# Half-token products after Strassen's scheme in a gated feed-forward block

## The chip, the cores and the metric

One core of a Trainium2 chip runs the whole program. The metric is the device time of one execution in microseconds. The engines that matter are TensorE (PE, with its weight loads, PEld), VectorE (DVE), ScalarE (ACT) and SyncE (SP), which issues nearly all DMAs from one queue.

## What is computed

A decoder trunk of one layer: 512 tokens, width 1024. Four attention branches are mixed and added to `x`; then comes the part that is changed:

```python
def conv_ffn(xn, w_up, conv_w, conv_b, w_down):
    hdn = xn @ w_up                               # 512 x 1024 times 1024 x 5632
    hp = jnp.pad(hdn, ((0, 0), (CONV_W - 1, 0), (0, 0)))
    acc = conv_b
    for j in range(CONV_W):                       # causal, over tokens, width 3
        acc = acc + conv_w[j] * hp[:, j:j + s_len]
    g, u = jnp.split(acc, 2, axis=-1)
    return (jax.nn.gelu(g, approximate=False) * u) @ w_down   # 512 x 2816 times 2816 x 1024
x = x + conv_ffn(rmsnorm(x, norm_ffn_g), ...)
return rmsnorm(x, norm_final_g)
```

## The kernel before, in words

Everything is held transposed: channels on the 128 partitions, the 512 tokens on the free axis. A float32 product is made of float32r parts: each operand is split into a high part (a cast, on ACT) and a low part (raw minus high, on DVE), and a product is three matmuls, high by high, high by low and low by high.

**The weight stream.** All big weights are entries of one list, `stream`, in the order in which PE wants them. `emit_weight` (L93) loads an entry of up to 128x1024 into a raw buffer (tag `wr`, two buffers, DMA on SP) and splits it into a high and a low tile (tags `wh` and `wl`, three buffers each) with `split_weight` (L89: cast on ACT, subtract on DVE). `weight()` (L106) returns the next entry and emits entries until two beyond it are there. Emitted weights get a priority 60 instructions ahead of their place.

**Order of the work.** PE's instructions stay in the order of the program. Those of the other engines are placed by a planner by priority, which is the place in the program, and by readiness: a ready instruction may pass one that waits. The buffers of one tag, though, are handed out in the order in which the program asks for them, each as soon as any buffer of the tag is free, which is when all that use the tile in it are done.

**Up projection** (44 tiles of 128 output channels). `up_tile(i)` (L798) runs 24 matmuls of 512 columns (L120: eight blocks of contraction times three) into a PSUM bank (tag `a`, six banks), DVE multiplies by the norm's factor into `h` (L805, two buffers), ACT makes the first tap and the bias (`cv`, L807, three buffers), DVE adds two taps (L809). Tiles come in pairs, gate and value: ACT takes the gate's gelu (L815), DVE multiplies (L817), and ACT and DVE split the product into `mh` and `ml` (L818, L819), which hold 22 blocks for the down projection.

**Down projection** (8 tiles). For each, `weight(3, 1)` gives the 22 blocks of contraction in entries of 8, 8 and 6 (`DCH`), and `down` (L829) runs 66 matmuls of 512 columns (L833). DVE adds the result to `x1` (L854), ACT squares it (L856), DVE sums the squares in `accf` (L858), ACT applies the gain (L859). The last tile runs in two halves of 256 tokens, 66 matmuls of 256 columns each. `last_norm` (L839) makes each half's factor from the squares and multiplies the outputs (L845), which four DMAs a half write (L846). That of the first half is issued within the second half's matmuls.

Of the kernel before, what the change touches and what calls it, by code (L numbers as in the profile page):

```python
# [44 lines left out]
def fr(ap):  # L45
    return ap.bitcast(F32)
# [3 lines left out]
def trunk(ctx: ExitStack, tc: tile.TileContext, xt, wv0, wv, wp, wdk, wg, wb, wo, wu, wd,  # L50
          convp, foxb, t5, onehot, consts, ymask, out):
    nc = tc.nc
    V, A, G, T, SP = nc.vector, nc.scalar, nc.gpsimd, nc.tensor, nc.sync
# [3 lines left out]
    wpool = ctx.enter_context(tc.tile_pool(name="wpool", bufs=WBUFS))  # L57
    xpool = ctx.enter_context(tc.tile_pool(name="xpool", bufs=1))
# [28 lines left out]
    stream, ready = [], []  # L87
# [90 lines left out]
    with ExitStack() as ph:  # L178
# [23 lines left out]
        rstd = cp.tile([P, S], F32, name="rstd0")  # L202
# [32 lines left out]
        for c, (a, b) in list(enumerate(CHUNKS))[1:]:  # L235
            sq = hp.tile([P, 2, S], F32, name=f"sq{b}", tag="sq", bufs=4)
# [46 lines left out]
        for tt in range(NB):  # L283
            jk = pp.tile([P, P], F32, name=f"jk{tt}", tag="ot")
            V.tensor_tensor_reduce(out=jk, in0=rstd[:, tt * P:(tt + 1) * P], in1=ident, scale=1.0, scalar=0.0,
                                   op0=OP.mult, op1=OP.add, accum_out=rst[:, tt:tt + 1])
        for tt in range(NB):
# [3 lines left out]
                            op0=OP.mult)  # L291
# [87 lines left out]
        with tc.issue_after(last_lo):  # L379
# [16 lines left out]
                             op0=OP.mult, op1=OP.add)  # L396
        ch = pp.tile([P, 2, S], F32R, name="ch", tag="hi", bufs=HB)
# [241 lines left out]
        for pr in ("F0", "S0", "F1", "S1", "M0", "M1", "D0", "D1"):  # L639
            nm, b = pr[0], "FMSD".index(pr[0])  # L640
            for h in (2 * int(pr[1]), 2 * int(pr[1]) + 1):
                q = lambda pr=pr: qk[pr + "q"]
                if nm == "D":
                    k, v = (lambda: kD[:, 0]), (lambda: vvD[:, :, 0])
                else:
                    k = lambda pr=pr, hh=h % 2: qk[pr + "k"][:, hh]
# [3 lines left out]
                else:  # L650
                    bias = fox_bias if nm == "F" else t5_bias(h + 4 * (nm == "D"), nm == "D")
# [115 lines left out]
        for f in range(KT):  # L767
            ps = bank(f"o{f}")
# [25 lines left out]
    mh = p3.tile([P, ND, S], F32R, name="mh")  # L794
    ml = p3.tile([P, ND, S], F32R, name="ml")
    rstd = None

    def up_tile(i):  # L798
        nonlocal rstd
        ps = bank(f"u{i}")  # L800
        drive(dense_steps(ps, *weight(), blocks_of(xhi), blocks_of(xlo), late=(i == 0)))
        if i == 0:
            rstd = rms_rstd(mean_square([acc], "mso"), S, "f", p3)
        h = p3.tile([P, S], F32, name=f"h{i}", tag="h", bufs=2)
        V.tensor_tensor(out=h, in0=ps, in1=rstd, op=OP.mult)  # L805
        c = p3.tile([P, S], F32, name=f"cv{i}", tag="cv", bufs=3)
        A.activation(c, h, AF.Identity, scale=cvp[:, i, 2:3], bias=cvp[:, i, 3:4])  # L807
        for x in (1, 2):
            V.scalar_tensor_tensor(out=c[:, x:], in0=h[:, :S - x], scalar=cvp[:, i, 2 - x:3 - x], in1=c[:, x:],  # L809
                                   op0=OP.mult, op1=OP.add)  # L810
        return c

    for j in range(ND):
        g = up_tile(2 * j)
        last_gelu = A.activation(g, g, AF.Gelu)  # L815
        u = up_tile(2 * j + 1)
        V.tensor_tensor(out=u, in0=g, in1=u, op=OP.mult)  # L817
        A.copy(mh[:, j], u)  # L818
        V.tensor_tensor(out=ml[:, j], in0=u, in1=fr(mh[:, j]), op=OP.subtract)  # L819
    with tc.issue_after(last_gelu.ins):  # L820
        A.preload_act_table_set("natural_log_exp_and_others")

# [3 lines left out]
    accf = p3.tile([P, S], F32, name="accf")  # L826
    full = slice(0, S)

    def down(ch, o, cs, late=False):  # L829
        blocks = [(hi[:, k], lo[:, k], k0 + k) for (hi, lo), (k0, c) in zip(ch, DCH) for k in range(c)]  # L830
        for n, (hi, lo, k) in enumerate(blocks):
            for m, (a, b) in enumerate(((hi, mh), (hi, ml), (lo, mh))):
                T.matmul(o, a, b[:, k, cs], start=(n == 0 and m == 0), stop=(n == ND - 1 and m == 2))  # L833
            if n % 4 == 3:
                yield

    msf = [None, None]

# [7 lines left out]
            (SP if q % 2 == 0 else A).dma_start(out[:, 2 * q:2 * q + 2, hs[h]], xs)  # L846

    for f in range(KT):
        ch = weight(3, 1)
        gf = gn[:, 2 * KT + f:2 * KT + f + 1]  # L850
        if f < KT - 1:
            ps = bank(f"dn{f}")
            drive(down(ch, ps, full))
            V.tensor_tensor(out=x1[f], in0=ps, in1=x1[f], op=OP.add)  # L854
            sq = p3.tile([P, S], F32, name=f"sqd{f}", tag="h", bufs=2)
            A.activation(accf if f == 0 else sq, x1[f], AF.Square)  # L856
            if f:
                V.tensor_tensor(out=accf, in0=accf, in1=sq, op=OP.add)  # L858
            A.activation(x1[f], x1[f], AF.Copy, scale=gf)  # L859
# [20 lines left out]
CHUNKS = ((0, 1), (1, 2), (2, 4), (4, 6), (6, 8))  # L880
WARM = 9
NV0 = 328
DCH = ((0, 8), (8, 8), (16, 6))
# [109 lines left out]
```

## Time and profile before

| | us |
|---|---|
| median of 3 runs | 857.08 (856.91 to 857.58) |
| the profiled execution | 857.41 |
| its span in the profile | 855.6 |
| PE busy | 837.3 |
| up projection, PE | 483.3 to 723.2 |
| down projection, PE | 723.2 to 845.4 |

The span runs from the first to the last instruction in the trace; the execution's own time has some 1.8 us around it. A line of a profile names the line of the code, the engine, the operation, output <- inputs by the program's names, and the shape (partitions x elements). "Idle before" is the time for which the engine stood before that instruction, and behind `<-` stands what ended it. Matmuls are pipelined, so PE's spacing is read from many in a row.

### The profile page before, as it was taken

Reading aid. Unit: us, or ns where it says so; the run is one execution under the profiler, and the core shown is the slowest. Engines: PE = TensorE matmul, PEld = TensorE weight load, DVE = VectorE, ACT = ScalarE, POOL = GpSimd, SP = SyncE. Lnnn points to the kernel's source line nnn. Section 1 sums busy time; section 2 is a strip of 40 time slices with the busy share of each in tenths; the row PEclk is TensorE's granted clock in tenths of the full one; section 3 lists DMA queues with packets and bytes.
Section 4 is the critical chain, followed back from the end, with each engine's and each line's share of the span. In section 5 each row is a group of like instructions: output and inputs, shape, how many; then the busy total and the mean of one; then the engine's idle time right before and its main releaser. Section 6 shows DMA issues by size and latency. Waiting matters only on the chain.

```text
span 855.6 us, 10625 instructions
## 1 busy us (share of the span) xinstructions
PE 837.3 (98%) x4019; PEld 702.2 (82%) x4019; DVE 538.1 (63%) x931; ACT 398.8 (47%) x612; POOL 164.6 (19%) x131
## 2 busy tenths in 40 slices
PE   8999999999999999999999999999999999999995
PEld 7778887888888888888888888888888888888885
DVE  5947899996453468455554477777777777333234
ACT  6556785664554843232344454444444444232231
POOL 1244575377568300000001200000000000000000
PEclk9999999999999999999999999999999999999998
DMA  6567334326332243232223223333333333333322
GB/s 227 167 163 178 100 132 108 87 58 189 90 120 74 75 130 117 74 103 96 77 74 107 89 98 98 99 99 99 98 99 99 98 97 91 90 93 93 90 65 98
DMA packets 31667, 90.68 MB, mean 106 GB/s; under 512 B 3384, under 2 KB 8376, under 8 KB 31616
## 3 DMA queue, kind: packets, MB, share of 16 engines
q1 hardware_dynamic: 30240, 88.62, 34.3%
q10 hardware_dynamic: 1376, 1.38, 0.5%
q8 instruction: 31, 0.51, 0.2%
q14 instruction: 20, 0.16, 0.1%
HBM read 83.78 MB, written 5.82 MB: 105 GB/s over the span
## 4 chain that ended last, share of the span: by engine, by line
PE 80%; DVE 1%; POOL 0%; ACT 0%; issue 0%; DVEq 0%; POOLq 0%
PE u L120 28%; PE dg L120 19%; PE dn L833 14%; PE o L120 5%; PE b L120 5%; PE vpsVM L303 1%; PE dM1q L120 1%; PE dM1k L120 1%; PE zb L545 1%; PE dD1q L120 1%; PE dD0q L120 1%; PE ptD L484 1%; PE ptM L484 1%; PE dM0q L120 0%; PE oD L500 0%; PE oM L500 0%
## 5 line engine op out<-in xcount | busy, mean ns | idle before, releaser
L90 ACT CAST wh<-wr 128x1024 fp32r<-128x1024 f32 (+1 forms) x129 | 133.7, 1039 | 153.8 <-PE dn L833 70.4
L91 DVE TENSOR_TENSOR wl<-wr,wh 128x1024 fp32r<-128x1024 f32 (+2 forms) x97 | 116.3, 1200 | 138.6 <-ACT wh L90 63.6
L120 PE MATMUL u<-xhi,wh 128*128 128x512 f32 x352 | 87.5, 390 | 0.0
L91 POOL TENSOR_TENSOR wl<-wr,wh 128x1024 fp32r<-128x1024 f32 x32 | 77.0, 2408 | 52.9 <-PE dix L120 15.3
L120 PE MATMUL u<-xlo,wh 128*128 128x512 f32 x352 | 87.1, 389 | 0.0
L120 PE MATMUL u<-xhi,wl 128*128 128x512 f32 x352 | 87.1, 389 | 0.0
L809 DVE SCALAR_TENSOR_TENSOR cv<-h,cvp,cv 128x511 f32<-128x511 f32 x88 | 66.0, 751 | 26.2 <-ACT cv L807 24.6
L120 PEld LDWEIGHTS u<-xhi,wh 128*128 128x128 f32 x352 | 66.1, 188 | 14.1 <-issue 0.5
L120 PEld LDWEIGHTS u<-xlo,wh 128*128 128x128 f32 x352 | 66.1, 188 | 13.7
L120 PEld LDWEIGHTS u<-xhi,wl 128*128 128x128 f32 x352 | 66.1, 188 | 13.7
L807 ACT ACTIVATE cv<-h,cvp 128x512 f32<-128x512 f32 x44 | 35.9, 815 | 79.8 <-DVE h L805 79.8
L833 PE MATMUL dn<-mh,wh 128*128 128x512 f32 (+1 forms) x198 | 72.9, 368 | 0.0
L833 PE MATMUL dn<-ml,wh 128*128 128x512 f32 (+1 forms) x198 | 72.3, 365 | 0.0
L833 PE MATMUL dn<-mh,wl 128*128 128x512 f32 (+1 forms) x198 | 72.3, 365 | 0.0
L120 PE MATMUL dg<-xlo,wh 128*128 128x512 f32 x256 | 66.1, 392 | 0.0
L120 PE MATMUL dg<-xhi,wh 128*128 128x512 f32 x256 | 64.9, 390 | 0.0
L120 PE MATMUL dg<-xhi,wl 128*128 128x512 f32 x256 | 64.3, 390 | 0.0
L120 PEld LDWEIGHTS dg<-xhi,wl 128*128 128x128 f32 x256 | 47.7, 188 | 9.8
L120 PEld LDWEIGHTS dg<-xhi,wh 128*128 128x128 f32 x256 | 47.8, 188 | 9.4
L120 PEld LDWEIGHTS dg<-xlo,wh 128*128 128x128 f32 x256 | 47.4, 188 | 9.5
L781 POOL TENSOR_TENSOR rstd<-rstd,sqo 128x512 f32<-128x512 f32 x7 | 9.1, 1302 | 187.1 <-ACT sqo L780 187.1
L833 PEld LDWEIGHTS dn<-ml,wh 128*128 128x128 f32 x198 | 37.3, 188 | 6.2
(430 smaller groups left out, 1453.0 us busy)
## 6 DMA issues: line engine op xcount, KB each, us to landing
wr<-in_wu SPq DMA_DIRECT2D x44, 512.0 KB
wr<-in_wg SPq DMA_DIRECT2D x32, 512.0 KB
wr<-in_wp SPq DMA_DIRECT2D x16, 512.0 KB
wr<-in_wd SPq DMA_DIRECT2D x16, 512.0 KB
wbr<-in_wb SPq DMA_DIRECT2D x8, 512.0 KB
wr<-in_wo SPq DMA_DIRECT2D x8, 512.0 KB
wr<-in_wd SPq DMA_DIRECT2D x8, 384.0 KB
bdram<-brd SPq DMA_DIRECT2D x2, 1280.0 KB
```

What stands on the lines that cost most here:

```text
L90: A.copy(hi, raw)
L91: eng.tensor_tensor(out=lo, in0=raw, in1=fr(hi), op=OP.subtract)
L120: T.matmul(o, a[:, k], b(k), start=(n == 0), stop=(n == len(todo) - 1))
L303: T.matmul(ps, a[:, k, ts_], b, start=(m == 0), stop=(m == 3 * KT - 1))
L484: T.transpose(pt[:, (i - j) * P:(i - j + 1) * P], z[:, QOFF[i] + P * j:QOFF[i] + P * (j + 1)], ident)
L545: T.matmul(zs[j][:, P * (j2 - j):n], trir if j2 == j else negr, x[:, KOFF[j2]:KOFF[j2] + n2], start=False, stop=(j2 == NB - 1 and x is ll) ...
L781: G.tensor_tensor(out=acc, in0=acc, in1=sq, op=OP.add)
L807: A.activation(c, h, AF.Identity, scale=cvp[:, i, 2:3], bias=cvp[:, i, 3:4])
L809: V.scalar_tensor_tensor(out=c[:, x:], in0=h[:, :S - x], scalar=cvp[:, i, 2 - x:3 - x], in1=c[:, x:], op0=OP.mult, op1=OP.add)
L833: T.matmul(o, a, b[:, k, cs], start=(n == 0 and m == 0), stop=(n == ND - 1 and m == 2))
```

## The change

Two weight tiles (a pair of up tiles, or two down tiles), eight blocks of contraction in two groups of four, and two halves of 256 tokens make a product of 2x2 by 2x2 blocks. The kernel after takes it with seven products of sums in place of eight products, in Winograd's form, for the up pairs j = 5, 8, 11 and 13 and, in the down projection, for the first eight blocks of tiles (0,1), (2,3), (4,5) and (6,7). One such product is 12 matmuls of 256 columns. Between the products of a unit stands the work of another tile (`rest`): the 24 matmuls of the next up tile, or the 42 matmuls of the down projection's blocks 8 to 21 of one tile. In the down projection, tiles 0 to 2 do their blocks 8 to 21 first; the units come with tiles 3 to 6, and tile 7 ends in halves as before, with 14 blocks.

The sums of weights are made on DVE after both raw tiles are loaded. The differences of the moving operand are made once: `tu` from the normed `x1` (for the up units), `tq` from `mh` + `ml` (for the down units), in buffers that other tiles use before or after.

```diff
+    def unit_weights(src1, src2, nm, pool):
...
+        def first():
+            r1, r2 = (wpool.tile([P, 1024], F32, name=f"ur{nm}{x}", tag="wr", bufs=RBUFS) for x in range(2))
+            ws = pool().tile([P, 1024], F32, name=f"ws{nm}", tag="ws", bufs=1)
+            box.update(r1=r1, r2=r2, ws=ws)
+            SP.dma_start(r1, src1)
+            SP.dma_start(r2, src2)
+            ts = pair(0)
+            split_weight(r1, *ts, V)
...
+        def second():
...
+            V.tensor_tensor(out=ws[:, :512], in0=r2[:, :512], in1=r2[:, 512:], op=OP.add)
+            V.tensor_tensor(out=ws[:, 512:], in0=ws[:, :512], in1=r1[:, :512], op=OP.subtract)
+            ts = pair(1)
+            split_weight(ws, *ts, V)
...
+        def third():
...
+            V.tensor_tensor(out=r2[:, :512], in0=r1[:, :512], in1=r2[:, :512], op=OP.subtract)
+            ts = pair(2, True)
+            split_weight(r2, *ts, V)
...
+        def fourth():
...
+            V.tensor_tensor(out=ws[:, :512], in0=r1[:, 512:], in1=ws[:, 512:], op=OP.subtract)
+            ts = pair(3)
+            split_weight(ws[:, :512], ts[0][:, :512], ts[1][:, :512], V)
...
+    def product(o, w, at, xh, xl, first, last):
+
+        for k in range(4):
+            for m, (a, b) in enumerate(((w[0], xh), (w[0], xl), (w[1], xh))):
+                T.matmul(o, a[:, at + k], b(k), start=(first and k == 0 and m == 0), stop=(k == 3 and m == 2),
+                         skip_group_check=True)
...
+            stream += [u[0], u[1], (wu[i + 2], (KT, P), V), u[2], u[3]]
...
+            ws = [u[0], u[1], ws[0], u[2], ws[1], u[3]]
...
+    def x1_differences(k):
+        xg = p3.tile([P, 2, S], F32, name=f"xg{k}", tag="ws")
+        for x in range(2):
+            f = k + 4 * x
+            A.activation(xg[:, x], x1[f], AF.Copy, scale=gn[:, KT + f:KT + f + 1])
+        t = p3.tile([P, 4, HALF], F32, name=f"xt{k}", tag=("uh", "ul")[k % 2])
+        differences(xg[:, 0], xg[:, 1], t[:, 0:2], t[:, 2:4])
+        A.copy(tu[0][:, k], t)
+        V.tensor_tensor(out=tu[1][:, k], in0=t, in1=fr(tu[0][:, k]), op=OP.subtract)
...
+        q1, q2, q5 = (bank(f"un{n}{x}")[:, :HALF] for x in range(3))
+        wa, wsum = weight(2)
+        product(q1, wa, 0, *quad(0, 0), True, True)
+        yield 0, 0, True, q1
+        product(q2, wa, 4, *quad(4, 0), True, True)
+        yield 0, 0, False, q2
+        product(q5, wsum, 0, *diff(0), True, True)
+        yield 1, 1, True, q5
+        next(rest)
+        product(q1, wsum, 4, *diff(1), False, True)
+        yield 0, 1, True, q1
+        wd3 = weight()
+        next(rest)
+        product(q1, wd3, 0, *diff(2), False, True)
+        yield 1, 1, False, q1
+        drive(rest)
+        product(q5, weight(), 0, *quad(4, 1), False, True)
+        yield 0, 1, False, q5
+        product(q1, wd3, 4, *diff(3), False, True)
+        yield 1, 0, None, q1
...
+        middle(j, g, u)
+        if 0 < j < 5:
+            x1_differences(j - 1)
...
+    tq = [xpool.tile([P, 4, 4, HALF], F32R, name=f"tq{x}", tag=x) for x in ("xh", "xl")]
+    for k in range(4):
+        m1, m2 = (p3.tile([P, S], F32, name=f"mm{k}{x}", tag="h", bufs=2) for x in range(2))
+        ta, tb = (p3.tile([P, 2, HALF], F32, name=f"tt{k}{x}", tag="cv", bufs=3) for x in range(2))
+        for m, kk in ((m1, k), (m2, k + 4)):
+            V.tensor_tensor(out=m, in0=fr(mh(kk)), in1=fr(ml(kk)), op=OP.add)
+        differences(m1, m2, ta, tb)
+        for x, t in enumerate((ta, tb)):
+            d = slice(2 * x, 2 * x + 2)
+            A.copy(tq[0][:, k, d], t)
+            V.tensor_tensor(out=tq[1][:, k, d], in0=t, in1=fr(tq[0][:, k, d]), op=OP.subtract)
...
+UNITS = (5, 8, 11, 13)
+NA = 14
```

`pair(2, True)` gives a tile of its own (tags `uh` and `ul`, one buffer each), the other pairs are of `wh` and `wl`. `differences` is four DVE subtractions of 256 tokens. What a product yields is taken from the bank at once: in the up units by an ACT copy (first into that quarter) or by a DVE add, and a DVE multiply by the norm's factor at a quarter's end; in the down units by a DVE add to `x1`. The up rest yields after 12 and 18 of its 24 matmuls, the down rest after 24 and 33 of its 42. `mh` and `ml` are cut in two tiles each (`NA` blocks and the rest), so that the second can use the buffer of `tu`.

## Rows read from the trace of the kernel before

**Rows 1.** The page: the span, and PE's busy time, share and instructions.

```profile
span 855.6 us, 10625 instructions
...
PE 837.3 (98%) x4019; PEld 702.2 (82%) x4019; DVE 538.1 (63%) x931; ACT 398.8 (47%) x612; POOL 164.6 (19%) x131
```

**Rows 2.** The page: the chain that ended last, by engine and by line.

```profile
PE 80%; DVE 1%; POOL 0%; ACT 0%; issue 0%; DVEq 0%; POOLq 0%
PE u L120 28%; PE dg L120 19%; PE dn L833 14%; PE o L120 5%; PE b L120 5%; PE vpsVM L303 1%; PE dM1q L120 1%; PE dM1k L120 1%; PE zb L545 1%; PE dD1q L120 1%; PE dD0q L120 1%; PE ptD L484 1%; PE ptM L484 1%; PE dM0q L120 0%; PE oD L500 0%; PE oM L500 0%
```

**Rows 3.** Windows, the up and the down stage: length, then busy us (count) by engine.

```profile
core 0: us, PE busy (x) PEld busy (x) DVE busy (x) ACT busy (x) POOL busy (x), PEclk, DMA share, GB/s
483.30:723.20 239.90, 239.90 (x1058) 198.28 (x1057) 174.78 (x220) 109.81 (x135) 1.29 (x1) 1.00 0.31 96
723.20:845.40 122.20, 122.18 (x602) 103.76 (x600) 41.03 (x49) 34.10 (x42) 0.00 (x0) 1.00 0.28 83
```

**Rows 4.** The chain in order of time, merged: start, us, engine, tile, line, count.

```profile
489.66 233.93 PE u L120 x1032
...
833.05 6.46 PE dn L833 x54
```

**Rows 5.** Groups by form in the up stage, 540 to 720: count, busy us, mean ns, idle before.

```profile
L91 DVE TENSOR_TENSOR wl<-wr,wh 128x1024 fp32r<-128x1024 f32 x33 | 40.4, 1225 | 27.0 <-PE u L120 27.0
L90 ACT CAST wh<-wr 128x1024 fp32r<-128x1024 f32 x33 | 34.8, 1056 | 29.5 <-PE u L120 29.5
...
L809 DVE SCALAR_TENSOR_TENSOR cv<-h,cvp,cv 128x511 f32<-128x511 f32 x33 | 24.8, 751 | 19.6 <-ACT cv L807 19.6
...
L805 DVE TENSOR_TENSOR h<-u,yf 128x512 f32<-128x512 f32 x34 | 23.2, 683 | 0.0
L817 DVE TENSOR_TENSOR cv<-cv,cv 128x512 f32<-128x512 f32 x17 | 11.8, 693 | 0.6
```

**Rows 6.** Groups by form in the down stage, 723 to 846.

```profile
L833 PEld LDWEIGHTS dn<-mh,wl 128*128 128x128 f32 x198 | 37.3, 188 | 6.1
...
L91 DVE TENSOR_TENSOR wl<-wr,wh 128x768 fp32r<-128x768 f32 x8 | 7.7, 959 | 1.2 <-PE u L120 1.2
...
L870 DVE TENSOR_TENSOR x<-dn,x 128x256 f32<-128x256 f32 x2 | 0.8, 425 | 6.7 <-PE dn L833 6.7
...
L872 ACT ACTIVATE sqe<-x 128x256 f32<-128x256 f32 x2 | 0.8, 417 | 11.6 <-DVE x L870 11.6
...
L818 ACT CAST mh<-cv 128x512 fp32r<-128x512 f32 x1 | 0.6, 621 | 2.3 <-DVE cv L817 2.3
```

**Rows 7.** Groups by form on ACT, 440 to 490.

```profile
L773 ACT ACTIVATE xhi<-x,cst 128x512 fp32r<-128x512 f32 x8 | 5.8, 723 | 18.4 <-DVE x L771 18.4
```

**Rows 8.** Waits of SP's DMA queue from 500 us on: total, times, longest.

```profile
SPq L100 <- DVE wl L91: 299.3, 61, 6.2
```

**Rows 9.** Timeline of SP, then of ACT: a load of 512 KB and its cast.

```profile
302.07 2.15 SPq L723 DMA_DIRECT2D wbr<-in_wb  x2
...
305.74 1.05 ACT L90 CAST bh<-wbr 128x1024 fp32r<-128x1024 f32 x1 [3.87 <-DMA wbr<-in_wb]
```

**Rows 10.** Timeline of DVE at the change of stage: start, length, operation, [idle before].

```profile
723.68 0.96 DVE L91 TENSOR_TENSOR wl<-wr,wh 128x768 fp32r<-128x768 f32 x1 [1.19 <-PE u L120]
...
729.08 0.69 DVE L819 TENSOR_TENSOR ml<-cv,mh 128x512 fp32r<-128x512 f32 x1 [0.69 <-ACT mh L818]
```

**Rows 11.** Timeline of DVE at the end.

```profile
842.33 2.48 DVE L845 TENSOR_TENSOR x<-x,msf 128x512 f32<-128x512 f32 x4
845.42 0.42 DVE L870 TENSOR_TENSOR x<-dn,x 128x256 f32<-128x256 f32 x1 [0.61 <-PE dn L833]
```

**Rows 12.** Timeline of PE at the start; then windows at the end, columns as in rows 3.

```profile
1.32 4.16 PE L200 MATMUL wps<-warm 128*128 128x512 f32 x9 [1.32 <-POOL warm L186]
...
847.40:848.00 0.60, 0.00 (x0) 0.00 (x0) 0.00 (x0) 0.57 (x2) 0.00 (x0) 1.00 0.00 0
848.50:849.00 0.50, 0.00 (x0) 0.00 (x0) 0.47 (x2) 0.00 (x0) 0.00 (x0) 0.50 0.00 0
```

More of the change, by code (lines that the diff above doesn't have):

```diff
@@ L93, in emit_weight @@
     def emit_weight():
+        if callable(stream[len(ready)]):
+            with tc.high_priority(offset=PRIO):
+                ready.append(stream[len(ready)]())
+            return
         src, shape, eng = stream[len(ready)]
@@ L793, in trunk, with mid @@
     p3 = ctx.enter_context(tc.tile_pool(name="p3", bufs=1, reuse_waits="tile"))
[L794 to L796 removed]
+    pools["p3"] = p3
+    tu = [p3.tile([P, 4, 4, HALF], F32R, name=f"tu{x}", tag=x) for x in ("mbh", "mbl")]
+    ma = [p3.tile([P, NA, S], F32R, name=f"{x}a") for x in ("mh", "ml")]
+    mb = []
+    def mid(x):
+        return lambda k: ma[x][:, k] if k < NA else mb[x][:, k - NA]
+    mh, ml = mid(0), mid(1)
@@ new lines, in trunk, with up_tail, differences @@
+    rstd = None
+    def up_tail(i, h):
+        c = p3.tile([P, S], F32, name=f"cv{i}", tag="cv", bufs=3)
+        A.activation(c, h, AF.Identity, scale=cvp[:, i, 2:3], bias=cvp[:, i, 3:4])
+        for x in (1, 2):
+            V.scalar_tensor_tensor(out=c[:, x:], in0=h[:, :S - x], scalar=cvp[:, i, 2 - x:3 - x], in1=c[:, x:],
+                                   op0=OP.mult, op1=OP.add)
+        return c
+    def differences(b1, b2, ta, tb):
+        V.tensor_tensor(out=ta[:, 0], in0=b1[:, hs[1]], in1=b1[:, hs[0]], op=OP.subtract)
+        V.tensor_tensor(out=ta[:, 1], in0=b2[:, hs[1]], in1=ta[:, 0], op=OP.subtract)
+        V.tensor_tensor(out=tb[:, 0], in0=b2[:, hs[1]], in1=b1[:, hs[1]], op=OP.subtract)
+        V.tensor_tensor(out=tb[:, 1], in0=b2[:, hs[0]], in1=ta[:, 1], op=OP.subtract)
@@ L803, in up_tile, with evicted @@
             rstd = rms_rstd(mean_square([acc], "mso"), S, "f", p3)
+        return up_tail(i, evicted(i, ps))
+    def evicted(i, ps):
         h = p3.tile([P, S], F32, name=f"h{i}", tag="h", bufs=2)
         V.tensor_tensor(out=h, in0=ps, in1=rstd, op=OP.mult)
[L806 to L810, printed above, removed]
@@ L811, in up_tile, with up_rest @@
-        return c
-    for j in range(ND):
[L814 to L819, printed above, removed]
+        return h
+    def up_rest(i, box):
+        ps = bank(f"u{i}")
+        hi, lo = weight()
+        todo = [(a, b, k) for a, b in ((hi, xhi), (hi, xlo), (lo, xhi)) for k in range(KT)]
+        for n, (a, b, k) in enumerate(todo):
+            T.matmul(ps, a[:, k], b[:, k], start=(n == 0), stop=(n == len(todo) - 1))
+            if n in (11, 17):
+                yield
+        box.append(ps)
@@ new lines, in up_unit @@
+    def up_unit(j, box):
+        hg, hu = (p3.tile([P, S], F32, name=f"hu{j}{x}", tag="h", bufs=2) for x in range(2))
+        h2 = (hg, hu)
+        for x, h, first, q in unit_of(f"u{j}", (lambda k: xhi[:, k], lambda k: xlo[:, k]), tu, up_rest(2 * j + 2, box)):
+            d, r = h2[x][:, hs[h]], rstd[:, hs[h]]
+            if first:
+                A.copy(d, q)
+            elif first is None:
+                V.tensor_tensor(out=d, in0=q, in1=r, op=OP.mult)
+            else:
+                V.tensor_tensor(out=d, in0=d, in1=q, op=OP.add)
+                V.tensor_tensor(out=d, in0=d, in1=r, op=OP.mult)
+        return hg, hu
@@ new lines, in middle @@
+    def middle(j, g, u):
+        V.tensor_tensor(out=u, in0=g, in1=u, op=OP.mult)
+        A.copy(mh(j), u)
+        V.tensor_tensor(out=ml(j), in0=u, in1=fr(mh(j)), op=OP.subtract)
+    ahead = {}
+    for j in range(ND):
+        if j == NA:
+            mb += [p3.tile([P, ND - NA, S], F32R, name=f"{x}b", tag=t) for x, t in (("mh", "mbh"), ("ml", "mbl"))]
+        if j in UNITS:
+            box = []
+            h2 = up_unit(j, box)
+            ahead[2 * j + 2] = box[0]
+            g = up_tail(2 * j, h2[0])
+            last_gelu = A.activation(g, g, AF.Gelu)
+            u = up_tail(2 * j + 1, h2[1])
+        else:
+            i = 2 * j
+            g = up_tail(i, evicted(i, ahead[i])) if i in ahead else up_tile(i)
+            last_gelu = A.activation(g, g, AF.Gelu)
+            u = up_tile(2 * j + 1)
+        middle(j, g, u)
+        if 0 < j < 5:
+            x1_differences(j - 1)
@@ L827, in trunk, with down @@
     full = slice(0, S)
-    def down(ch, o, cs, late=False):
+    def down(ch, o, cs):
         blocks = [(hi[:, k], lo[:, k], k0 + k) for (hi, lo), (k0, c) in zip(ch, DCH) for k in range(c)]
@@ L832, in down, with down_unit, rest_of, finished_tile @@
             for m, (a, b) in enumerate(((hi, mh), (hi, ml), (lo, mh))):
-                T.matmul(o, a, b[:, k, cs], start=(n == 0 and m == 0), stop=(n == ND - 1 and m == 2))
+                T.matmul(o, a, b(k)[:, cs], start=(n == 0 and m == 0), stop=(n == len(blocks) - 1 and m == 2))
             if n % 4 == 3:
                 yield
+    tq = [xpool.tile([P, 4, 4, HALF], F32R, name=f"tq{x}", tag=x) for x in ("xh", "xl")]
[9 more added lines that the diff above has]
+            V.tensor_tensor(out=tq[1][:, k, d], in0=t, in1=fr(tq[0][:, k, d]), op=OP.subtract)
+    def down_unit(n, rest):
+        for x, h, _, q in unit_of(f"d{n}", (mh, ml), tq, rest):
+            d = x1[n + x][:, hs[h]]
+            V.tensor_tensor(out=d, in0=d, in1=q, op=OP.add)
+    def rest_of(f):
+        ps = bank(f"dn{f}")
+        n = 0
+        blocks = []
+        for g in range(2):
+            hi, lo = weight()
+            c = DCH[g][1]
+            for k in range(c):
+                for m, (a, b) in enumerate(((hi, mh), (hi, ml), (lo, mh))):
+                    T.matmul(ps, a[:, k], b(DCH[g][0] + k), start=(g == 0 and k == 0 and m == 0),
+                             stop=(g == 1 and k == c - 1 and m == 2))
+                if g == 1 and k == 2:
+                    yield
+            if g == 0:
+                yield
+        V.tensor_tensor(out=x1[f], in0=ps, in1=x1[f], op=OP.add)
+    def finished_tile(f):
+        gf = gn[:, 2 * KT + f:2 * KT + f + 1]
+        sq = p3.tile([P, S], F32, name=f"sqd{f}", tag="h", bufs=2)
+        A.activation(accf if f == 0 else sq, x1[f], AF.Square)
+        if f:
+            V.tensor_tensor(out=accf, in0=accf, in1=sq, op=OP.add)
+        A.activation(x1[f], x1[f], AF.Copy, scale=gf)
     msf = [None, None]
@@ L848, in trunk @@
     for f in range(KT):
[L849 to L859, printed above, removed]
-        else:
+        if f < 3:
+            drive(rest_of(f))
+        elif f < KT - 1:
+            n = 2 * (f - 3)
+            down_unit(n, rest_of(f))
+            finished_tile(n)
+            if n + 1 < KT - 1:
+                finished_tile(n + 1)
+        else:
+            ch = weight(2, 1)
+            gf = gn[:, 2 * KT + f:2 * KT + f + 1]
             pend = None
```

43 lines of the change are left out of this document (38 added, 5 removed).

## The prediction

> **What bounds the kernel now.** I read the page's busy shares first: TensorE (PE) is busy 837.3 of 855.6 us [rows 1]. The chain that ended last says the same of the path: 80% TensorE, with the up projection (L120, u) 28% and the down projection (L833, dn) 14% [rows 2]. Then the two stages that are changed, as windows: in the up stage, 483.3 to 723.2, PE is busy for all 239.90 us and VectorE (DVE) for 174.78; in the down stage, 122.18 of 122.20 and 41.03 [rows 3]. So here the time is the number of matmuls times their spacing, as long as nothing makes PE wait. The merged chain gives the spacing: 1032 matmuls of 512 columns in 233.93 us are 226.7 ns each; 54 of 256 columns in 6.46 us are 119.6 ns each [rows 4]. Half the columns cost 53% of the time, and the fixed part is about 13 ns a matmul.
>
> **What the change takes away.** A unit pairs two weight tiles over eight contraction blocks. It took 48 matmuls of 512 columns, 48 x 226.7 = 10.88 us; it takes 7 x 12 = 84 of 256 columns, 84 x 119.6 = 10.05 us. That is 0.83 us, not an eighth (1.36 us). Eight units (four up, four down) give 6.6 us. The last down tile ran its first eight blocks at 256 columns, 48 x 119.6 = 5.74 us in place of the 5.44 I counted, so 0.3 more: **-6.9 us**. The weight loads don't stand in the way: each matmul of that stretch has a load of its own, whose row reads 188 ns [rows 6], and yet they follow at 119.6.
>
> The Trainium skill ("TensorE: Matmul & The Clock Gate", section Back-to-back issue gap) gives an isolated gap of columns over 2.4 plus 2.5 ns. By it a unit would go from 10.36 to 9.17 us, and the eight would save 9.5. The trace disagrees (226.7, not 215.8 ns), and the measurement decides.
>
> **What it adds on DVE and ACT.** From the rows by form: the low half of a 1024-wide weight takes DVE 1.225 us and its cast ACT 1.056; 512-wide element-wise work is 0.683 to 0.693, the two convolution taps 0.751 each [rows 5]. A 768-wide low half takes 0.959, a 256-wide operation 0.425 on DVE and 0.417 on ACT, a 512-wide cast 0.621 [rows 6].
> An up unit: three low halves of 1024 and one of 512, and four sums of 512, 7.1 us where 2.45 stood; seven 256-wide evictions, 3.0 us for 1.4. So 6.3 us more DVE work per unit. A pair of tiles costs 8.15 us of DVE now per 10.88 us of PE, so in a unit with its neighbour tile DVE has 12.2 + 6.3 = 18.5 us of work in 15.5 us of PE. A backlog of 3 us comes, which the tiles between units (a quarter idle) clear; six PSUM banks cover it. Cost zero, if only evictions and convolutions are late; 3 us a unit if that cover fails.
> The differences of x1, 2.9 us of DVE four times, have no data to wait for and run early in idle time, but for one buffer, next.
>
> **Wait 1, in the first up unit (j=5).** Tile `ws` has one buffer and goes to its users in the order of the program. `weight()` runs two entries ahead, so `first` of unit 5 is emitted in tile 8 (j=4), before x1_differences(3), which stands behind middle(4) and takes `ws` too. So the fourth k of `tu` is made only when unit 5's `fourth` has split `ws`, and `fourth` needs the weight buffer that the first two products release, 2.87 us into the unit. From there, in a row: ACT cast 0.62, DVE 0.69, two ACT copies with scale 0.72 each [rows 7], three differences 1.28, ACT cast 1.06, DVE 1.23, and hand-overs of some 0.05: ready at 9.4. The third product wants it at 4.07. PE waits **+5.3 us** (4.5 to 5.5; 0 if the order is not so).
>
> **Smaller waits in the up units.** The third use of bank q1 has 6 matmuls, 1.36 us, to let ACT copy it (0.42). At the same moment a weight buffer falls free and its cast (1.06) may stand first: 0.3 us a unit. Unit 13 follows unit 11 with one tile between and its raw weights come late by half a us or so. I take **+1.2** (0 to 4).
>
> **Wait 2, at the change of stage.** `tq` needs 8 sums of 512, 16 differences and 8 low halves of 512: 5.5 + 6.8 + 5.5 = 17.8 us of DVE. Its scratch tiles share `h` and `cv` with the up tiles, again in program order, so nothing of it starts before the last up tile. Cover: tiles 0 to 2 of the contraction's rest, 126 x 0.2267 = 28.6 us, then 36 half matmuls, 4.31: at 32.9 PE wants the first eight-block weight behind the first down unit. That weight needs a raw buffer, of which there are two, held by the unit's r1 and r2 until `third` or `fourth` is through. The weight stream already waits for raw buffers: SP stood 299.3 us for DVE's low halves in 61 issues [rows 8]. Before r2 falls free DVE has: last up tile 3.6, weights 1.2 + 1.2 + 1.0 + 1.2 + 1.0, `second` 2.6, `third` 1.9, `tq` 17.8, one eviction 0.7: 32.2 us without a gap. Then the load, 3.67 us from issue (302.07) to the cast that waited for it (305.74) [rows 9], cast 1.06, low half 1.23: ready at 38.2 and wanted at 33.3, 4.9 us late; with idle DVE between (1.19 us before the first, 0.69 in the tail of the last up tile [rows 10]) about 7; 3.7 if `fourth` goes before `third`. I take **+5.5**. The tail of the last up tile ended at 729.8, 6.6 us after the change of stage [rows 10], and is wanted at 9.1 now, not 14: covered, unless tq's work pushes in front.
>
> **Wait 3, in down units 2 to 4.** `uh` and `ul` have one buffer: `third` of a unit can only be split when the unit before has ended, so r2 stays. r1 stays until `fourth` has subtracted, behind `second`'s split, which gets its weight buffer 2.9 us before the unit begins: cast 1.06, low half 1.23, eviction 0.43, subtract 0.69: 0.5 us into the unit. Load 3.67, cast 1.06, low half 1.23: 6.5. PE wants it at 4.31 + 0.45 = 4.76. So 1.7 us (1.3 to 2.5), three times: **+5.1**.
>
> **The end.** The four closing multiplies of the first half run 842.33 to 844.81, and the last add comes at 845.42, just behind them [rows 11]. The second half loses 24 half matmuls, 2.87 us, so the add is ready at 842.55. Behind the multiplies it is 2.2 us late, before them 0.3. No row shows the order; I take the middle, **+1.2**.
>
> Weights' bytes are the same, the loads move within SP's one queue; POOL gets nothing.
>
> **The sum.** -6.9 + 5.3 + 1.2 + 5.5 + 5.1 + 1.2 = +11.4 us. The profiled execution took 857.4 us around its span of 855.6; the median of the runs is 857.1, 0.3 below. So 868.8 on its base, **868.5 us** as a median.
>
> **Rivals.**
> *Covered (faster).* Place: DVE's idle time, 65 us in the up stage and 81 in the down stage [rows 3]. All that is added is some 85 us (4 x 6.3, 4 x 2.9, 17.8, and 4 x 7.5 in the down units: 5.9 for weights and 1.6 for evictions), so by the averages it fits, the buffers come free in time and PE never waits. Price: -6.9 and at most the end's 1.2 back, 851.4 us by the median. It decides if the waits together stay under 5.2 us. Against it: the averages don't see that one-buffer tiles and the program's order tie the work to a moment. Chance 0.13.
> *One wait only (same).* Wait 1 forms, the stage change finds its cover and the raw buffers come free early: -6.9 + 5.3 + 1.2, 856.7. Chance 0.07.
> *The clock falls in the waits (slower still).* With PE done, the granted clock is still full, 2.4 GHz, from 847.4 to 848 and half, 1.2, from 848.5; nine matmuls of 512 columns at the start took 4.16 us [rows 12], where nine at 226.7 ns and a drain of 0.16 are 2.2. If PE restarts so after waits 1 and 2, each costs 2 us more: 872.5. The Trainium skill (the same page, Part 1: The HAM clock gate) says too that a clock at half rate is the idle state. Chance 0.16.
> *DVE's backlog reaches PE.* The 3 us of each up unit become waits: 12 us for 1.2, 879. For it: 18.5 in 15.5 us; against it six banks. Chance 0.08.
> That the change doesn't do what it says I give nothing: the matmuls it issues are counted in the code.
>
> **How the numbers follow.** The forecast has 0.56; with the two that are slower still, slower is 0.80. About 0.2%, 1.7 us, is what a measurement of this kernel can tell from no change. Faster 0.13, same 0.07. The waits' low ends (4.5, 0, 3.7, 3.9, 0.3) give +5.5, 862.6; the high ends (5.5, 4, 7, 7.5, 2.2) +19.3, 876.4. The range goes from 856, which takes in the case of one wait, to 877; left out are the covered case and the backlog.
>
> **What would show it.** Right: spacing near 120 ns in the units; PE idle 5 us in unit 5 at its third product, released by the differences' low half; a gap of 5 us or so in the first down unit and of 1 to 2 in the three later ones, each at the first full-width matmul behind the third product, with SP waiting for DVE. Wrong: no such gaps; x1's differences all done before unit 5; tq's sums running before the last up tile; or half-token matmuls above 125 ns.

## The result, and the profile after

The change makes the kernel slower: **869.06 us** (868.48 to 869.54, 4 runs) beside 857.33 for the kernel before on the same chip, a ratio of 1.0134 [1.0118, 1.015]. The profiled execution took 869.29 us around a span of 867.5, so the span grew by 11.9 us.

The page of the kernel after: span, busy time by engine, PE's slices with the granted clock, and the chain by engine. It answers to [rows 1, 2].

```profile
span 867.5 us, 11389 instructions
...
PE 837.7 (97%) x4283; PEld 711.3 (82%) x4283; DVE 608.0 (70%) x1079; ACT 425.3 (49%) x660; POOL 164.6 (19%) x131
...
PE   8999999999999999999999999799999999999995
...
PEclk9999999999999999999999999799999999999998
...
PE 71%; DVE 6%; DMA 2%; ACT 2%; issue 1%; POOL 0%; DVEq 0%; ACTq 0%; SPq 0%; POOLq 0%
```

PE is busy as long as before although it has less to do, and its share of the chain fell from 80% to 71%; DVE, DMA and ACT came in. The 26th slice shows where: PE and its clock both drop to 7 tenths.

By stage, the windows of the kernel after, columns as in [rows 3]: the up stage, the down stage and what follows the last matmul but two.

```profile
482.72:731.32 248.60, 241.80 (x1203) 204.77 (x1203) 202.30 (x284) 126.86 (x168) 1.29 (x1) 0.98 0.29 93
731.32:856.92 125.60, 120.69 (x720) 106.33 (x719) 80.89 (x129) 43.64 (x57) 0.00 (x0) 1.00 0.26 78
856.92:867.50 10.58, 0.70 (x2) 0.30 (x2) 6.75 (x13) 1.31 (x3) 0.00 (x0) 0.75 0.60 198
```

The windows of [rows 3] set the change of stage of the kernel before at 723.2, a little early. Its merged chain has it at 723.59, in the way in which 731.32 is read here (start, us, engine, tile, line, count):

```profile
483.35 5.45 PE u L120 x24
...
723.59 109.03 PE dn L833 x498
```

So bounded, the up stage is 8.36 us longer (248.60 for 240.24), the down stage 3.79 (125.60 for 121.81), and the end 0.38. The up stage began 0.63 earlier. 8.36 + 3.79 + 0.38 - 0.63 = 11.9. The program ahead of the up stage is the same in all these kernels, and yet their profiles have its start anywhere from 482.07 to 484.71; no experiment asks why. What PE waited for from 480 us on (total, times, longest, in us):

```profile
PE unu L161 <- ACT tumbh L903: 5.5, 1, 5.5
PE dn L1046 <- ACT wh L90: 2.8, 4, 0.9
PE dn L1046 <- DVE wl L91: 2.1, 4, 0.5
```

One long wait in one up unit (`unu`), four short ones in the four down units, each at L1046, the first full-width matmul behind the third product. Those are the places forecast. The sizes are another matter.

**Unit 5.** Timeline of PE (start, length, operation, idle before and what ended it):

```profile
547.48 0.58 PE L161 MATMUL unu<-tumbh,uwhu 128*128 128x256 f32 x1 [5.53 <-ACT tumbh L903]
548.74 0.58 PE L161 MATMUL unu<-tumbl,uwhu 128*128 128x256 f32 x1 [0.68 <-DVE tumbl L904]
...
549.33 3.61 PE L956 MATMUL u<-xhi,wh 128*128 128x512 f32 x8
```

And the merged chain of the kernel after, for unit 5 and then for unit 8 (start, us, engine, tile, line, count):

```profile
549.53 5.12 PE u L956 x12
...
579.85 4.31 PE unu L161 x36
584.16 2.75 PE u L956 x12
```

Undisturbed, three products take 4.31 us and the neighbour tile's first twelve matmuls 2.75, as unit 8 shows. In the timeline unit 5 began at 537.84, so those twelve should have begun at 542.15. They began at 549.33 there, 7.2 us late, and took 2.4 longer (5.12 for 2.75). Why longer, the windows say (length, busy by engine, then the granted clock, third number from the right):

```profile
549.00:550.00 1.00, 1.00 (x4) 0.90 (x5) 0.94 (x1) 0.37 (x1) 0.00 (x0) 0.50 0.00 0
...
555.00:556.00 1.00, 1.00 (x11) 1.00 (x10) 0.00 (x0) 0.00 (x0) 0.00 (x0) 1.00 0.00 0
```

PE is busy in both, but at half clock (1.2 GHz) in the first: four matmuls start there. At 555 the clock is full again. All of unit 5 with its neighbour took 25.50 us (537.84 to 563.34), where 84 x 119.6 ns + 24 x 226.7 ns = 15.49: **10.0 us lost**.

Who held the differences up is read from DVE and ACT in that stretch:

```profile
541.09 1.23 DVE L91 TENSOR_TENSOR wl<-wr,wh 128x1024 fp32r<-128x1024 f32 x1
542.23 0.41 DVE L971 TENSOR_TENSOR hu<-hu,unu 128x256 f32<-128x256 f32 x1
542.57 0.69 DVE L976 TENSOR_TENSOR cv<-cv,cv 128x512 f32<-128x512 f32 x1
543.17 0.68 DVE L91 TENSOR_TENSOR uwlu<-wsu,uwhu 128x512 fp32r<-128x512 f32 x1
...
547.46 1.22 DVE L904 TENSOR_TENSOR tumbl<-xt,tumbh 128x1024 fp32r<-128x1024 f32 x1 [1.11 <-ACT tumbh L903]
```

```profile
541.23 0.62 ACT L90 CAST uwhu<-wsu 128x512 fp32r<-128x512 f32 x1
...
543.89 1.33 ACT L900 ACTIVATE xg<-x,cst 128x512 f32<-128x512 f32 x2
```

`fourth` was cast by 541.85, but its low half began at 543.17, behind a weight's low half, an eviction and a gate multiply. It ended at 543.85, and only then was `ws` free for `xg`, which began at 543.89. The last low half ended at 548.68, 10.84 us into the unit.

**The change of stage.** DVE of the kernel after, from the first weight behind the last up tile to `third`'s low half in the first down unit:

```profile
731.41 1.23 DVE L91 TENSOR_TENSOR wl<-wr,wh 128x1024 fp32r<-128x1024 f32 x1 [1.46 <-PE u L180]
732.56 0.68 DVE L947 TENSOR_TENSOR h<-u,yf 128x512 f32<-128x512 f32 x1
733.16 0.68 DVE L1024 TENSOR_TENSOR mm<-mha,mla 128x512 f32<-128x512 f32 x1
...
739.60 0.69 DVE L1024 TENSOR_TENSOR mm<-mha,mla 128x512 f32<-128x512 f32 x1
740.20 0.68 DVE L1029 TENSOR_TENSOR tqxl<-tt,tqxh 128x512 fp32r<-128x512 f32 x1
...
758.83 1.22 DVE L91 TENSOR_TENSOR uld<-urd,uhd 128x1024 fp32r<-128x1024 f32 x1
759.97 0.69 DVE L1052 TENSOR_TENSOR x<-dn,x 128x512 f32<-128x512 f32 x1
```

No row in this stretch has idle time before it but the first: DVE is the queue on which everything waits. The lengths of its 48 operations add up to 32.0 us, but the stretch lasts 28.56 (731.41 to 759.97). A 512-wide operation is 0.68 to 0.69 us long, and the next one starts 0.60 after it began (739.60, 740.20).

What follows, from SP's timeline (first row) and the merged chain:

```profile
760.08 2.13 SPq L104 DMA_DIRECT2D wr<-in_wd  x2
```

```profile
764.00 1.05 ACT wh L90
765.07 1.24 DVE wl L91
766.35 5.28 PE dn L1046 x22
...
781.79 3.45 DMA wr<-in_wd
...
787.62 5.28 PE dn L1046 x22
...
808.95 5.29 PE dn L1046 x22
...
830.43 5.28 PE dn L1046 x22
```

`third` done at 760, load, cast, low half, PE: that is wait 2. Wait 3 has the same chain from the load on, but there the load, at 781.79, follows `fourth`'s subtraction (DVE, ended at 781.72):

```profile
781.04 0.68 DVE L150 TENSOR_TENSOR wsd<-urd,wsd 128x512 f32<-128x512 f32 x1
```

A down unit is 84 x 119.6 ns and 42 x 226.7 ns, 19.57 us; from one eight-block stretch to the next it is 21.27, 21.33 and 21.48: 1.7, 1.8 and 1.9 us lost.

**The end.** The first half's add (L1095) now stands before its four multiplies (L1071), and holds them up by 0.34 us; compare [rows 11].

```profile
856.95 0.42 DVE L1095 TENSOR_TENSOR x<-dn,x 128x256 f32<-128x256 f32 x1 [0.25 <-PE dn L1013]
857.29 2.47 DVE L1071 TENSOR_TENSOR x<-x,msf 128x512 f32<-128x512 f32 x4
```

### The profile page after: what moved, and what is told of

Its sections match the earlier page's. It is cut to its first block, busy times and chain, and to the rows that moved or that the text cites. A ratio compares the mean times of both kernels' runs of the same rounds, so it can differ in the third digit from the quotient of the medians.

```text
span 867.5 us, 11389 instructions
## 1 busy us (share of the span) xinstructions
PE 837.7 (97%) x4283; PEld 711.3 (82%) x4283; DVE 608.0 (70%) x1079; ACT 425.3 (49%) x660; POOL 164.6 (19%) x131
## 4 chain that ended last, share of the span: by engine, by line
PE 71%; DVE 6%; DMA 2%; ACT 2%; issue 1%; POOL 0%; DVEq 0%; ACTq 0%; SPq 0%; POOLq 0%
PE u L180 19%; PE dg L180 19%; PE dn L1046 6%; PE o L180 5%; PE b L180 5%; PE unu L161 4%; PE u L956 3%; DMA wr<-in_wd 2%; PE und L161 2%; PE dn L1013 1%; PE vpsVM L377 1%; DMA wr<-in_wu 1%; DVE uwld L91 1%; DVE wl L91 1%; PE dM1q L180 1%
## 5 line engine op out<-in xcount | busy, mean ns | idle before, releaser
L90 ACT CAST wh<-wr 128x1024 fp32r<-128x1024 f32 (+2 forms) x113 | 116.7, 1036 | 104.8 <-PE dg L180 21.3
L91 DVE TENSOR_TENSOR wl<-wr,wh 128x1024 fp32r<-128x1024 f32 (+2 forms) x81 | 96.8, 1196 | 75.5 <-PE dg L180 27.1
L180 PE MATMUL u<-xhi,wh 128*128 128x512 f32 x256 | 63.9, 391 | 0.0
L180 PE MATMUL u<-xhi,wl 128*128 128x512 f32 x256 | 63.4, 389 | 0.0
L180 PE MATMUL u<-xlo,wh 128*128 128x512 f32 x256 | 63.4, 389 | 0.0
L885 DVE SCALAR_TENSOR_TENSOR cv<-h,cvp,cv 128x511 f32<-128x511 f32 (+1 forms) x72 | 53.3, 748 | 9.7 <-ACT cv L883 9.0
L180 PEld LDWEIGHTS u<-xhi,wh 128*128 128x128 f32 x256 | 47.8, 188 | 10.2 <-issue 0.5
L519 DVE MAX8 m<-isc 128x8 f32<-128x512 f32 (+2 forms) x48 | 26.5, 556 | 1.0
L520 DVE MATCH_REPLACE8 isc<-m,isc 128x512 f32<-128x512 f32 (+2 forms) x48 | 26.0, 542 | 0.1
L947 DVE TENSOR_TENSOR h<-u,yf 128x512 f32<-128x512 f32 x36 | 24.4, 684 | 1.2 <-PE u L180 1.1
```

What stands on the lines that cost most here:

```text
L90: A.copy(hi, raw)
L180: T.matmul(o, a[:, k], b(k), start=(n == 0), stop=(n == len(todo) - 1))
L519: V.max(out=m8, in_=t)
L520: V.match_replace(out=t, in_to_replace=m8, in_values=t, imm_value=MARK)
```

## The experiments

Each edit is to the kernel after; each ratio is to the kernel before, with its interval. The kernel before came out at 857.4 to 857.5 us beside each of them, so their times are set against the 869.06 of the kernel after as they are.

**1. The differences of x1 emitted one pair of tiles earlier.** Then x1_differences(3) takes `ws` before unit 5's `first`.

```diff
         middle(j, g, u)
-        if 0 < j < 5:
-            x1_differences(j - 1)
+        if j < 4:
+            x1_differences(j)
```

> x1_differences(k) stands behind middle(k), k = 0 to 3, one pair earlier than in the changed kernel; nothing else is changed. So the fourth one asks for `ws` before unit 5 does. Theory (order of `ws`): PE's wait of 5.5 + 0.7 us in unit 5 goes, and with it the half clock behind it; unit 5 takes 15.5 us where it took 25.5, and the kernel 869.1 - 10.0 = 859 us. Rival (DVE is overloaded around unit 5, and the fourth differences would be late in any order): most of the wait stays, 866 us or more.

Measured 859.46 us (858.33 to 861.0), 1.0023 [1.0014, 1.0033]: 9.6 under the kernel after. The wait for `tumbh` is gone from the list and the down units' four stay (2.3 and 2.1 us). So the order of the program at one buffer is the cause of wait 1, and 9.6 to 10 us its whole price. The edit moves the differences' work on DVE and ACT as well as their turn at `ws`; that it was the buffer on which they waited is read from the trace above, where `xg` begins 0.04 us after the last reader of `ws` ends.

**2. A raw buffer of its own for the eight-block weight of the down units.** The load behind the third product then needs neither r1's nor r2's place; `accf` takes over `acc`'s tile to make room.

```diff
-            raw = wpool.tile([P, 1024], F32, name=f"wr{i}", tag="wr", bufs=RBUFS)
+            if own:
+                raw = pools["p3"].tile([P, 1024], F32, name=f"wx{i}", tag="wx", bufs=1)
+            else:
+                raw = wpool.tile([P, 1024], F32, name=f"wr{i}", tag="wr", bufs=RBUFS)
...
-            ws = [u[0], u[1], ws[0], u[2], ws[1], u[3]]
+            ws = [u[0], u[1], ws[0] + (True,), u[2], ws[1], u[3]]
...
-    accf = p3.tile([P, S], F32, name="accf")
+    accf = acc
```

> The eight-block weight behind the third product of a down unit gets a raw buffer of its own (tag wx, 4 KB, in place of accf's own buffer, which now uses the dead acc), so its load waits for neither r1 nor r2. Theory (raw buffers): the gap of about 1.9 us goes in all four down units, 869.1 - 7.4 = 861.7 us. Rival (DVE is too late with the unit's sums and splits, so that the wait moves to the next product that needs them): under 3 us gained, 866 us or more, with PE waiting on und in place of dn.

Measured 860.76 us (860.32 to 862.67), 1.0041 [1.0026, 1.0056]: 8.3 under the kernel after. All four waits at L1046 are gone, the wait for `tumbh` stays at 5.5. The stage's waits were 1.9 + 1.7 + 1.8 + 1.9 = 7.3. The other microsecond is, by the profile, the clock's: the same wait in unit 5, but the twelve matmuls behind it took 3.92 us, not 5.12. Windows of this kernel:

```profile
551.00:552.00 1.00, 1.00 (x3) 0.76 (x3) 0.00 (x0) 0.00 (x0) 0.00 (x0) 0.50 0.76 160
552.00:553.00 1.00, 1.00 (x6) 0.78 (x5) 0.00 (x0) 0.00 (x0) 0.00 (x0) 0.97 0.86 348
```

The clock came back at 552 here, and after 554 in the kernel after: one wait, two prices.

**3. Both edits.**

> The two edits together: differences one pair earlier, and a raw buffer of its own for the eight-block weight. If the two waits are separate the gains add: 869.1 - 10.0 - 7.4 = 851.7 us, 0.6 to 0.7% faster than the kernel before. If one of them hides the other or a new wait comes: above 855 us.

Measured 853.26 us (851.55 to 854.57), 0.9952 [0.9934, 0.997]: faster than before. From 480 us to the closing, PE waits once, 0.7 us for an eviction in unit 13. The two causes are separate and account for 15.8 us of the kernel after. The single gains are 9.6 and 8.3; with unit 5's clock, which is in both, counted once, some 16.9. That last microsecond is within the spread of the four runs.

**4. Unit 5's wait filled with matmuls.** 24 matmuls of 512 columns go to a spare bank that nothing reads, ahead of the k = 3 of unit 5's third product.

```diff
+    products = [0]
+
     def product(o, w, at, xh, xl, first, last):
+        products[0] += 1
         for k in range(4):
+            if products[0] == 3 and k == 3:
+                dm = bank("fill", "mm")
+                for _ in range(FILL):
+                    T.matmul(dm, xhi[:, 0, :P], xhi[:, 0], start=True, stop=True)
...
+FILL = 24
```

> Unit 5's wait is left as it is, but 24 matmuls of 512 columns into a spare bank, whose result nobody reads, stand in front of the fourth k of the third product: 5.4 us of work in the 5.5 us of wait. Theory (the granted clock falls in the wait, and that costs 2.4 us in the 12 matmuls behind it and 0.4 in others): granted clock 1.00 through 541 to 556 us, the 12 matmuls of the next tile in 2.7 us where they took 5.1, kernel 866 us. Rival (what follows the wait is slow for another reason, such as late operands): 869 us or more.

Measured 866.01 us (865.44 to 866.52), 1.0098 [1.0083, 1.0113]: 3.05 under the kernel after, by doing more. Timeline of PE in that kernel, then a window of it:

```profile
541.88 5.63 PE L166 MATMUL fill<-xhi 128*128 128x512 f32 x24
...
549.14 2.00 PE L963 MATMUL u<-xhi,wh 128*128 128x512 f32 x8
```

```profile
547.00:550.00 3.00, 2.10 (x10) 1.34 (x9) 2.44 (x2) 0.86 (x2) 0.00 (x0) 1.00 0.00 0
```

The differences are as late as ever (the next tile begins at 549.14), but the clock stays full and the tile's matmuls come at full pace. Unit 5 with its neighbour takes 22.63 us here (537.93 to 560.56) for 25.50. So its 10.0 us are 7.1 of waiting and 2.9 of a halved clock.

**5. tq's sums on POOL.** My reason: if DVE's queue sets wait 2, then eight operations fewer on it should take it away.

```diff
-            V.tensor_tensor(out=m, in0=fr(mh(kk)), in1=fr(ml(kk)), op=OP.add)
+            G.tensor_tensor(out=m, in0=fr(mh(kk)), in1=fr(ml(kk)), op=OP.add)
```

> The changed kernel with the eight sums mh + ml of tq on POOL in place of DVE; nothing else is changed. Theory (at the change of stage DVE's queue, in start-to-start times of some 0.60 us for 512 columns, sets when r1 and r2 fall free): 4.8 us leave DVE's queue, the load behind the first down unit is issued 2 us or more earlier, the gap of 1.9 us in that unit goes, and the three later ones stay at 1.7 to 1.9: 867.2 us. Rival (the chain of raw buffers sets it, as in the later units, whatever DVE has to do): all four gaps stay, 869 us.

Measured **874.07 us** (873.44 to 875.38), 1.0192 [1.0174, 1.0211]: 5.0 slower than the kernel after, and both theories missed. Timelines of POOL and of DVE in that kernel:

```profile
738.17 1.88 POOL L1024 TENSOR_TENSOR mm<-mha,mla 128x512 f32<-128x512 f32 x1 [0.94 <-DVE tt L893]
...
744.58 1.41 POOL L1024 TENSOR_TENSOR mm<-mha,mla 128x512 f32<-128x512 f32 x1 [2.50 <-DVE tt L893]
```

```profile
738.81 1.52 DVE L894 TENSOR_TENSOR tt<-mm,tt 128x256 f32<-128x256 f32 x1
...
744.76 2.31 DVE L91 TENSOR_TENSOR wl<-wr,wh 128x1024 fp32r<-128x1024 f32 x1
```

The low half at 744.76 takes 2.31 us where its kind takes 1.22: POOL's sum ends at 745.99, and 745.99 + 1.22 is 747.21, within 0.14 of its end. The 256-wide difference at 738.81 takes 1.52 for 0.42: 740.05 + 0.42 = 740.47, and it ends at 740.33. So a DVE operation with two inputs in SBUF that begins beside such a POOL operation does its work only when POOL is through, and the time that the sums no longer take on DVE goes into waiting. The Trainium skill ("SBUF — State Buffer", section SBUF: two separate sides) has the rule: the two engines share a port pair as an exclusive lock held for the whole instruction. The trace agrees in these two rows. The first down unit's eight-block stretch began 38.1 us after the change of stage, not 35.0. PE had by then waited 2.1 us at a stretch, and within the 22 matmuls that followed its clock fell to half: they took 6.88 us for 5.28. 3.1 + 1.6 = 4.7 of the 5.0. A window of the same kernel:

```profile
770.00:772.00 2.00, 2.00 (x6) 1.60 (x5) 0.84 (x2) 0.00 (x0) 0.00 (x0) 0.50 0.82 256
```

**6. No sums at all.** The differences of `tq` are taken from `mh` alone; the low part is left out of them. This asks what 5 was meant to ask, without POOL.

```diff
-        m1, m2 = (p3.tile([P, S], F32, name=f"mm{k}{x}", tag="h", bufs=2) for x in range(2))
...
-            V.tensor_tensor(out=m, in0=fr(mh(kk)), in1=fr(ml(kk)), op=OP.add)
...
-        differences(m1, m2, ta, tb)
+        differences(fr(mh(k)), fr(mh(k + 4)), ta, tb)
```

> The changed kernel with the eight sums mh + ml of tq left out: the differences are taken of mh alone, so the low part of the moving operand's differences is left out of the result. DVE has eight operations of 512 less at the change of stage, 8 x 0.60 = 4.8 us by their start-to-start times, and POOL gets nothing. Theory (DVE's queue sets the load behind the first down unit): that load is issued 2 us or more earlier, the gap of 1.9 us in the first down unit goes, the three later ones stay: 867.2 us. Rival (the chain of raw buffers sets it whatever DVE has to do): all four gaps stay, 869 us.

Measured 866.27 us (865.64 to 866.87), 1.01 [1.0083, 1.0117]: 2.8 under the kernel after. SP's timeline, then the merged chain of that kernel:

```profile
756.12 2.19 SPq L104 DMA_DIRECT2D wr<-in_wd  x2
```

```profile
763.32 5.47 PE dn L1046 x24
```

The load is issued at 756.12, not 760.08, and the first down unit goes from its third product (36 matmuls in 4.31 us from 759.01) into the eight blocks without a gap. The later three keep theirs (1.8 and 1.6 us over three units). Wait 2 hangs on the sums in DVE's queue, wait 3 does not. 1.9 of the 2.8 are wait 2's; some 0.5 came from unit 5, whose twelve matmuls took 4.58 us this time.

**7 and 8. Each half of the change alone**, with its mended order. Down units alone (the edit of 2, no units in the up stage, no differences of x1):

```diff
-        if 0 < j < 5:
-            x1_differences(j - 1)
...
-UNITS = (5, 8, 11, 13)
+UNITS = ()
```

> The down units alone, with the raw buffer of their own: no up unit (UNITS empty) and no differences of x1. Theory (the half-token products give what their matmuls save where nothing waits): 857.4 - 3.6 + 0.4 at the end = 854.2 us, PE without a wait in the down stage. Rival (the weights' and sums' work costs more than the trace of the waits shows): 856 us or more.

Up units alone (the edit of 1, the down stage as before the change):

```diff
-        if 3 <= f < KT - 1:
-            n = 2 * (f - 3)
-            u = unit_weights(wd[n, :, :1024], wd[n + 1, :, :1024], f"d{n}", lambda: pools["p3"])
-            ws = [u[0], u[1], ws[0], u[2], ws[1], u[3]]
...
-DCH = ((8, 8), (16, 6))
+DCH = ((0, 8), (8, 8), (16, 6))
```

> The up units alone, differences one pair earlier as in e1, and the down projection as in the kernel before (22 blocks, no tq). Theory: 857.4 - 3.3 + 1.8 of small waits (0.24 in three units, 1.1 in the last) = 855.9 us. Rival (DVE's 18.5 us of work in 15.5 us reaches PE): 858 us or more.

Measured 853.98 us (852.63 to 856.13), 0.9959 [0.9944, 0.9973] for the down units, with no wait of PE in either stage; 856.1 (855.66 to 857.29), 0.998 [0.9971, 0.9989] for the up units, with one of 0.5. Beside 857.5 for the kernel before that is -3.5 and -1.4. By my count four down units save 3.6, with the last tile's 0.3, and 0.4 goes at the end: the down half gives that, as near as its runs tell. Four up units save 3.3, and the up half loses 1.9 of it to its smaller waits (0.24 in three units, 1.1 in unit 13; next section).

**9. Both mended, and the last two up units one pair further apart.** Units 11 and 13 had one tile between them; units 10 and 13 have three.

```diff
-        if 0 < j < 5:
-            x1_differences(j - 1)
+        if j < 2:
+            x1_differences(2 * j)
+            x1_differences(2 * j + 1)
...
-UNITS = (5, 8, 11, 13)
+UNITS = (4, 7, 10, 13)
```

> Both mends of e3, and up units at j = 4, 7, 10 and 13, three pairs apart, in place of 5, 8, 11 and 13; the differences of x1 all stand in the first two pairs. Theory (the last unit's wait comes from the one tile that stands between units 11 and 13, in which DVE's backlog isn't cleared): PE's wait of 0.7 us for hu and its late restart go, 1.1 to 1.5 us under e3. Rival (the wait for hu is the order on ACT, which any unit can have): the time of e3, 853.3 us, with that wait in another unit.

With the edit of 2 as well: **851.41 us** (851.31 to 852.77), 0.9929 [0.9915, 0.9943], the fastest of all and 6.1 us under the kernel before. The wait in unit 13 went from 0.7 to 0.3. Against experiment 3 the intervals overlap, so the size of this last step stays open. The merged chain of this kernel, for its stages:

```profile
720.41 28.56 PE dn L1051 x126
...
838.22 0.72 PE dn L1018 x6
```

Its down stage, in which PE waits nowhere, takes 118.53 us (720.41 to 838.94) for 121.81 in the kernel before, 3.3 less; its up stage 238.34 (from 482.07) for 240.24, 1.9 less. 1.3 of the gain lies ahead of the up stage, where the program is the same.

## Why the prediction was right, and where it was not

The sum came to +11.4 us, and the span grew by 11.9. The direction and the places hold; that the number does is partly luck, since two terms failed in opposite directions. The measured terms add up to 12.4; the 0.6 by which the up stage began earlier, which no term covers, leaves 11.8.

| term | forecast, us | measured, us |
|---|---|---|
| matmuls saved | -6.9 | -6.9 by their spacing |
| wait 1, unit 5 | 5.3 | 10.0 |
| smaller waits in the up units | 1.2 | 1.6 |
| wait 2, change of stage | 5.5 | 1.9 |
| wait 3, down units 2 to 4 | 5.1 | 5.4 |
| the end | 1.2 | 0.4 |

- **What the change takes away: right.** Half-width matmuls follow at 0.12 us in the units (12 in 1.43 us). In experiment 9 the down stage gives 3.3 of its 3.6, and the up stage 1.9 of its 3.3 with 1.3 of smaller waits left in it (0.24 in three units, 0.6 in unit 13): nearly all is there. An eighth of the products is not an eighth of the time, since the fixed 13 ns a matmul come twice as often.
- **Wait 1: mechanism right, two sizes off.** Experiment 1 shows the order of `ws`. The step that failed is "from there, in a row": cast and low half of `fourth` do not follow each other when DVE has three operations before the second of them. Ready was 10.84 us into the unit, not 9.4. And the clock, 2.9 us, was left out of the likeliest case.
- **The rival "the clock falls in the waits": right for wait 1, not for wait 2.** I priced it at 2 us each; experiment 4 shows 2.9 for unit 5. Behind wait 2's two short halts (0.91 and 0.53 us) the 22 matmuls took 5.28 us, as in the later units. I had given one condition for both waits, and their lengths differ by a factor of four. Even with it, 5.3 + 2 would have been short of unit 5's 10.0.
- **Smaller waits: right in size.** Units 8 and 11 take 0.24 us more than 15.49 each. Unit 13 loses 1.1: there PE waits 0.6 for ACT's copy out of the bank, and ACT had stood 3.7 us for a weight load before the work ahead of that copy, so late weights, as argued, are part of it. By its own pieces, 0.3 in four units and half a us in unit 13, the forecast term is 1.7 and not 1.2. The rival of a DVE backlog (3 us a unit) did not come.
- **Wait 2: mis-sized, 5.5 for 1.9.** I added up 32.2 us of DVE work "without a gap", and the trace has 32.0: the operations were counted right. But lengths of records are not the spacing of operations: 28.56 us passed. Those 3.4 us are the error. Everything else stood as forecast: `tq`'s first sum after the last up tile's `h`, the load behind `third`, 3.9 us from there to the cast (760.08 to 764.00; forecast 3.67). Experiment 6 shows that DVE's queue is the cause.
- **Wait 3: right**, 1.7 forecast and 1.7 to 1.9 measured, by the chain named: r1 held until `fourth` has subtracted. Experiment 2 shows that the raw buffer is what it hangs on.
- **The end: 0.4 for 1.2.** The add went before the multiplies, the lower of my two bounds.
- **"Covered" and "one wait only" fell**, but experiment 3 is the covered case: by averages the work fits, and once two orders are changed it does. The averages were right about the amount of work, and silent about its order.

## What to carry to other kernels

Before work is moved off the bounding engine, list for each new operand the buffer that it needs and who holds that buffer at that moment in program order: here three such waits cost 10.0 + 1.9 + 5.4 = 17.3 us where 6.9 were to be had, and they went with one moved line and one more buffer. Add up a queue by the start-to-start distance of its operations, not by the length of their records. The waits of 5.5 and 2.1 us on TensorE (unit 5; experiment 5) cost their length and then the clock here; the halts of 0.9 us and less in the down units cost no clock.

## What was not expected of the hardware

- DVE's records overlap. In an unbroken queue, 48 operations with 32.0 us of recorded length passed in 28.56, some 0.07 us less for each. The Trainium skill ("Perfetto Trace Analysis", section on the DVE / Act engine instruction) says that a record runs to the acknowledgement of the write while the next operation may begin to read before that; this is its account, and the trace shows only the overlap.
- The return of the clock varies for the same wait of 5.5 us: the same twelve matmuls behind it took 5.12 us twice, 4.58 and 3.92 in the profiles of four kernels that are alike up to there (the kernel after and experiments 5, 6 and 2). The Trainium skill ("TensorE: Matmul & The Clock Gate", Part 1) says that the throttled state is the default and that activity releases it; the halved clock at the restart in unit 5 (0.50 from 549 to 550) agrees.
- Moving a two-input operation from DVE to POOL freed nothing: a 1.22 us operation became 2.31 us beside a 1.41 us sum on POOL.
